# Latent attention: the halves of a head's output copied to one place by ScalarE and added on GpSimd, in place of a matmul by a shift matrix

## The chip, the cores and the metric

The kernel runs on one core of a Trainium2 chip. The time is device time in microseconds (us); the median of three runs of the kernel before is 2149.26 us (2146.79 to 2149.29). Engines are named as in the profile: PE is the matmul engine and PEld its weight loads, DVE is VectorE, ACT is ScalarE, POOL is GpSimd, and SP issues most of the DMAs.

## The reference

The program computes two hybrid decoder layers on 1024 tokens. In each layer three groups of heads run side by side (a gated linear recurrence, latent attention, and cross-attention into 256 memory tokens). Each output is multiplied by a gate, all are put side by side and go through one output projection and a layer norm. The change touches the latent attention alone:

```python
def attend(args):
    qn, qr, blk = args
    s = (jnp.einsum('bqhd,bkhd->bhqk', qn, k_nope)
         + jnp.einsum('bqhr,bkr->bhqk', qr, k_rope)).astype(jnp.float32) * scale
    ...
    s = jnp.where(mask, s, NEG_BIG)
    p = jax.nn.softmax(s, axis=-1).astype(v.dtype)
    return jnp.einsum('bhqk,bkhd->bqhd', p, v)
...
y = jnp.concatenate([y_hg * jax.nn.silu(hg_gate),
                     y_mla * jax.nn.silu(mla_gate),
                     y_mem * jax.nn.silu(mem_gate)], axis=-1)
```

There are 8 heads with values of width 64, and the attention is causal.

## The kernel before, in words

The latent attention of a layer is the function `mla_attend`. It walks 32 steps, 8 heads by 4 pairs of query blocks (`j` = 0 to 3, 256 queries each), in one fixed order.

- `scores` of the next step is written ahead of the rest of a step. For each of the two 128-query blocks PE makes the scores in a PSUM tile A (there are two), DVE takes the row maximum (`nm`, L1041), ACT the exponential and its sum (`pr`, L1044), DVE the reciprocal of the sum (`rs`, L1045), and POOL scales the rows (`pr`, L1048), in chunks of up to 512 columns. A tile A is free for the next scores when its exponential is done.
- `turn` transposes 256 keys by 256 queries of `pr` on PE (L1058) into a PSUM tile B (there are four). ACT rounds them to `ph` (L297) and DVE takes the rest `pl` (L298), so that a product keeps its precision with two matmuls.
- `values` multiplies `ph` and `pl` with the values (L1082, L1083) into one tile B for the whole step. It runs three turns behind (`LAG`). The weights `VV` of a head hold the rounded values in columns 0 to 63 and what is left in columns 64 to 127, so the product holds two halves in partitions 0 to 63 and 64 to 127, and the output is their sum.
- `close` makes that sum. ACT copies the whole product to SBUF (`ol`, L1086, one buffer), and one turn later PE multiplies it with `shift` (L1093), a 128x128 matrix that moves partitions 64 to 127 down by 64, and adds it to the same PSUM tile. DVE multiplies the first 64 partitions with the gate (`yt`, L1096, two buffers), and SP stores the result to HBM (`Yd`, L1097). So each of the 64 steps of the two layers has one copy, one matmul by `shift`, one multiplication and one store.

In the second step of a head the next head's queries are projected (`qf`, then `qh` and `ql` on POOL, L1011 and L1012). Between the last step of a head and the third of the next stand the short steps `j` = 0 and 1, with few products between one score and the next. We call that stretch a head boundary. There are seven in a layer.

A scheduler orders the program: it takes each engine's instructions by their place in the code and by its own estimate of when they are ready. An engine runs its instructions in that order and waits where one is not ready. So removing or adding an instruction also moves others.

Of the kernel before, what the change touches and what calls it, by code (L numbers as in the profile page):

```python
# [7 lines left out]
F32 = mybir.dt.float32  # L8
F32R = mybir.dt.float32r
# [3 lines left out]
ALU = mybir.AluOpType  # L13
# [4 lines left out]
P = 128  # L18
# [23 lines left out]
C_ID = 0  # L42
# [39 lines left out]
def program(tc, xT, xtok, memT, pos, w_in, small, w_uq, w_uk, w_uv, w_mk, w_mv,  # L82
            w_out, ln_g, ln_b, cst, msk, out):
    nc = tc.nc
    es = ExitStack()

    def pool(name, **kw):
        return tc.tile_pool(name=name, **kw)

    cp = es.enter_context(pool("cp", bufs=1))  # L90
# [29 lines left out]
    def T(pl, shape, dt=F32, tag=None, bufs=None):  # L120
        n_name[0] += 1
        return pl.tile(shape, dt, tag=tag, name=f"{tag}_{n_name[0]}", bufs=bufs)
# [4 lines left out]
    def psB():  # L127
        return T(pss.p, [P, 512], F32, "B", 4)

    def f32(t):  # L130
        return t.bitcast(F32)
# [8 lines left out]
    NSM = small.shape[1]  # L140
    sm = T(cp, [P, NSM], F32, "sm")

    shift = T(cp, [P, P], F32R, "shift")
    mhalf = T(cp, [P, 8], F32, "mhalf")
    nc.gpsimd.memset(mhalf, -0.5)
    ones = T(cp, [P, 2], F32, "ones")
# [9 lines left out]
    def constants(lp):  # L156
        cs = T(wpc[1], [P, 2048], F32, "raw", 2)[:, 0:C_N]
        nc.scalar.dma_start(cs, cst)
        nc.scalar.dma_start(sm, small)
        nc.gpsimd.memset(f32(shift), 0.0)  # L160
        nc.scalar.copy(shift[:, 0:64], cs[:, C_ID + 64:C_ID + P])
        nc.scalar.copy(idr, cs[:, C_ID:C_ID + P])
        for i, c in enumerate((C_BE, C_BO)):
            nc.scalar.copy(bias_r[i], cs[:, c:c + P])
        mx = T(lp, [P, HGH], F32, "mx")
        nc.vector.tensor_tensor(out=mx, in0=sm[:, 0:8], in1=sm[:, 8:16], op=ALU.max)
        e = T(lp, [P, 2, HGH], F32, "e")
        for l in range(2):
            nc.vector.tensor_tensor(out=e[:, l], in0=sm[:, 8 * l:8 * l + 8], in1=mx, op=ALU.subtract)
        nc.scalar.activation(e, e, AF.Exp)  # L170
        sme = T(lp, [P, HGH], F32, "sme")
        nc.vector.tensor_tensor(out=sme, in0=e[:, 0], in1=e[:, 1], op=ALU.add)
        nc.vector.reciprocal(out=sme, in_=sme)
        for l in range(2):
            nc.vector.tensor_tensor(out=e[:, l], in0=e[:, l], in1=sme, op=ALU.mult)
        nc.vector.memset(lb[:, 0], 0.0)
        nc.vector.tensor_tensor(out=lb[:, 1], in0=e[:, 0], in1=e[:, 1], op=ALU.add)
        nc.vector.tensor_tensor(out=lb[:, 1], in0=lb[:, 1], in1=e[:, 0], op=ALU.subtract)
        nc.vector.tensor_scalar(out=oml, in0=lb, scalar1=-1.0, scalar2=1.0, op0=ALU.mult, op1=ALU.add)
        return cs  # L180
# [175 lines left out]
    def mem_attn(l, X, tiles, kp):  # L356
        kT, vT, _ = tiles
        with pool(f"m{l}", bufs=1, reuse_waits="tile") as mp:
# [70 lines left out]
            def begin():  # L429
# [45 lines left out]
                for hd in range(2):  # L475
                    part("q", KC - 2, (hd,))
                    part("q", KC - 1, (hd,))
                    evac("q", hd, accs["q", hd])
                mem_in(tiles, mp)
                cs = constants(mp)  # L480
                rope_angles(mp, cs)
                rope_rows(mp)
# [507 lines left out]
    def mla_attend(l, cqT, ckT, KK, uq, kv, k_proj, k_odd, v_proj, rtab, VV, kvr, uqr, lp, rp):  # L990
        uqh, uql = (t.rearrange("p (r c) -> p r c", r=2) for t in uq)
        gs = []
# [71 lines left out]
        opss = {}  # L1064

        def values(hd, j, cp_, ph, pl_):
            hp, ab = hd // 2, hd % 2
            rw = slice(64 * ab, 64 * ab + 64)
            if cp_ == 0:
                opss[hd, j] = psB()  # L1070
            ops = opss[hd, j][:, 0:256].rearrange("p (b q) -> p b q", b=2)
            for c in range(2):
                kb_ = 2 * cp_ + c
                st = P if c == 0 else -P
                w = VV[:, kb_, hd]
                if kb_ == 2 * j + 1:
                    ov, rh, rl = ops[:, 1], ph[:, 2 * P:3 * P], pl_[:, 2 * P:3 * P]
                else:
                    ov = ops
                    rh, rl = (bass.AP(tensor=t.tensor, offset=t.offset + (0 if c == 0 else 3 * P),  # L1080
                                      ap=[list(t.ap[0]), [st, 2], [1, P]]) for t in (ph[:, :], pl_[:, :]))
                nc.tensor.matmul(ov, lhsT=w, rhs=rh, start=kb_ == 0, stop=False)  # L1082
                nc.tensor.matmul(ov, lhsT=w, rhs=rl, start=False, stop=kb_ == 2 * j + 1)  # L1083
            if cp_ == j:
                t = T(lp, [P, 256], F32R, "ol", 1)
                nc.scalar.copy(t, opss[hd, j][:, 0:256])  # L1086
                return t

        def close(hd, j, t):
            hp, ab = hd // 2, hd % 2  # L1090
            rw = slice(64 * ab, 64 * ab + 64)
            ops = opss.pop((hd, j))
            nc.tensor.matmul(ops[:, 0:256], lhsT=shift, rhs=t, start=False, stop=True, skip_group_check=True)  # L1093
            s_ = slice(j * 256, (j + 1) * 256)
            yt = T(lp, [P, 256], F32, "yt", 2)
            nc.vector.tensor_tensor(out=yt[rw], in0=ops[0:64, 0:256], in1=gs[hp][rw, s_], op=ALU.mult)  # L1096
            (nc.gpsimd if hd == 7 and j > 1 else nc.sync).dma_start(Y[8 + hp, rw, s_], yt[rw])  # L1097

        q_proj(0)
# [10 lines left out]
        def step(a):  # L1110
            t = values(*a)
            if ends:
                close(*ends.pop())
            if t is not None:
                ends.append((a[0], a[1], t))
# [29 lines left out]
        if ends:  # L1145
            close(*ends.pop())
# [201 lines left out]
    for l in range(DEPTH):  # L1348
# [4 lines left out]
        ops = latents_out(l, X, tp)  # L1353
# [75 lines left out]
```

## Time and profile before

| What | Value |
|---|---|
| median of the runs | 2149.26 us |
| time of the profiled execution | 2147.82 us |
| its span | 2146.0 us |
| PE busy over the span | 2064.9 us (96%) |
| DVE busy | 1461.1 us (68%) |
| ACT busy | 1009.6 us (47%) |
| POOL busy | 375.5 us (17%) |
| first stage of latent attention | 729 to 890 us of the span |
| second stage | 1804 to 1965 us |

Matmuls are pipelined, so that one of 280 ns may be followed by the next after 120 ns; PE's cost is read from the starts, not from the sum of durations. The shares over the whole span say little about a stage of 161 us, so the stage is read by itself. The median of the runs is 1.44 us above the profiled execution's time.

### The profile page before, as it was taken

Reading aid. Unit: us, or ns where it says so; the run is one execution under the profiler, and the core shown is the slowest. Engines: PE = TensorE matmul, PEld = TensorE weight load, DVE = VectorE, ACT = ScalarE, POOL = GpSimd, SP = SyncE. Lnnn points to the kernel's source line nnn. Section 1 sums busy time; section 2 is a strip of 40 time slices with the busy share of each in tenths; the row PEclk is TensorE's granted clock in tenths of the full one; section 3 lists DMA queues with packets and bytes.
Section 4 is the critical chain, followed back from the end, with each engine's and each line's share of the span. In section 5 each row is a group of like instructions: output and inputs, shape, how many; then the busy total and the mean of one; then the engine's idle time right before and its main releaser. Section 6 shows DMA issues by size and latency. Waiting matters only on the chain. (4 is left out here: it accounts for less than half of the span.)

```text
span 2146.0 us, 30332 instructions
## 1 busy us (share of the span) xinstructions
PE 2064.9 (96%) x11176; PEld 1751.5 (82%) x11176; DVE 1461.1 (68%) x2663; ACT 1009.6 (47%) x1997; POOL 375.5 (17%) x524
## 2 busy tenths in 40 slices
PE   9998999999999899999999989999999998999997
PEld 7887888888888788788787878888888887888886
DVE  6536777777777788566764367777777777886524
ACT  5534443434343777444554344434343437775311
POOL 0212000000001445211101120000000014452202
PEclk9999999999999999999999999999999999999999
DMA  6413201111114301456761131111111134015312
GB/s 201 133 58 119 63 27 60 40 59 40 59 40 153 126 16 38 154 188 230 237 196 52 55 123 55 35 59 40 60 40 54 45 128 151 15 39 190 108 60 79
DMA packets 122100, 194.47 MB, mean 91 GB/s; under 512 B 8608, under 2 KB 90400, under 8 KB 121952
## 3 DMA queue, kind: packets, MB, share of 16 engines
q1 hardware_dynamic: 101488, 149.05, 21.4%
q0 software_dynamic: 8704, 28.58, 3.5%
q10 hardware_dynamic: 11760, 14.90, 2.1%
q8 instruction: 88, 1.44, 0.3%
q14 instruction: 60, 0.49, 0.1%
HBM read 151.09 MB, written 41.42 MB: 90 GB/s over the span
## 5 line engine op out<-in xcount | busy, mean ns | idle before, releaser
L271 PE MATMUL Y<-x,wh 128*128 128x512 f32 x576 | 234.4, 407 | 2.1 <-ACT wh L297 2.1
L273 PE MATMUL Y<-x,wl 128*128 128x512 f32 x576 | 232.9, 404 | 0.0
L272 PE MATMUL Y<-x,wh 128*128 128x512 f32 x576 | 228.3, 396 | 0.0
L252 DVE TENSOR_TENSOR wl<-raw,wh 128x512 fp32r<-128x512 f32 (+4 forms) x214 | 141.5, 707 | 85.0 <-ACT wh L251 84.8
L272 PE MATMUL Y<-t,wh 128*128 128x512 f32 x432 | 170.8, 395 | 0.0
L271 PE MATMUL Y<-t,wh 128*128 128x512 f32 x432 | 170.1, 394 | 0.5 <-ACT pt L710 0.5
L273 PE MATMUL Y<-t,wl 128*128 128x512 f32 x432 | 168.9, 391 | 0.0
L297 ACT CAST wh<-raw 128x512 fp32r<-128x512 f32 (+1 forms) x124 | 72.9, 593 | 192.5 <-DMA raw<-in_w_in 128.2
L251 ACT CAST wh<-raw 128x512 fp32r<-128x512 f32 (+4 forms) x214 | 118.2, 609 | 86.7 <-PE A L272 49.7
L297 ACT CAST wh<-S 128x512 fp32r<-128x512 f32 x144 | 89.0, 622 | 140.9 <-DVE S L695 65.5
L581 PEld LDWEIGHTS B<-Q,r 128*128 128x128 f32 x896 | 115.7, 191 | 38.4 <-issue 12.5
L1048 POOL TENSOR_SCALAR pr<-pr,rs 128x512 f32<-128x512 f32 (+1 forms) x192 | 116.8, 617 | 148.0 <-DVE rs L1045 135.1
L581 PE MATMUL B<-Q,r 128*128 128x128 f32 x896 | 132.2, 291 | 7.6 <-DVE Q L560 6.1
L298 DVE TENSOR_TENSOR pl<-B,ph 128x512 fp32r<-128x512 f32 (+1 forms) x192 | 119.6, 643 | 23.6 <-ACT ph L297 21.0
L298 DVE TENSOR_TENSOR wl<-raw,wh 128x512 fp32r<-128x512 f32 (+1 forms) x124 | 80.7, 655 | 75.4 <-ACT wh L297 74.6
L271 PEld LDWEIGHTS Y<-x,wh 128*128 128x128 f32 x576 | 109.6, 190 | 21.7 <-ACT wh L297 2.9
L273 PEld LDWEIGHTS Y<-x,wl 128*128 128x128 f32 x576 | 109.2, 190 | 21.3 <-DVE wl L298 1.2
L272 PEld LDWEIGHTS Y<-x,wh 128*128 128x128 f32 x576 | 109.5, 190 | 19.5
L1044 ACT ACTIVATE pr<-A,nm 128x128 f32<-128x128 f32 (+7 forms) x128 | 95.6, 748 | 60.8 <-DVE nm L1041 55.4
L297 ACT CAST ph<-B 128x512 fp32r<-128x512 f32 (+1 forms) x192 | 102.7, 553 | 32.0 <-PE B L1058 16.1
L271 PE MATMUL A<-wh,yh 128*128 128x512 f32 x288 | 112.6, 396 | 4.9 <-ACT wh L251 2.6
L298 DVE TENSOR_TENSOR yl<-yr,yh 128x768 fp32r<-128x768 f32 (+1 forms) x44 | 43.5, 997 | 106.9 <-ACT yh L297 106.0
(340 smaller groups left out, 5573.1 us busy)
## 6 DMA issues: line engine op xcount, KB each, us to landing
raw<-in_w_in SPq DMA_DIRECT2D x84, 512.0 KB, 4.6
raw<-in_w_out SPq DMA_DIRECT2D x32, 1024.0 KB, 5.2
yr<-Yd SPq DMA_DIRECT2D x28, 384.0 KB, 4.5
Yd<-r POOLq DMA_DIRECT2D x32, 256.0 KB, 2.6
raw<-in_w_mk SPq DMA_DIRECT2D x8, 512.0 KB, 4.9
raw<-in_w_mv SPq DMA_DIRECT2D x8, 512.0 KB, 4.4
t<-in_xT SPq DMA_DIRECT2D x16, 256.0 KB, 3.5
Yd<-yt POOLq DMA_DIRECT2D x16, 256.0 KB, 2.4
```

The costliest lines, as they stand in the source:

```text
L251: nc.scalar.copy(h[:, a:b], raw[:, a:b])
L252: nc.vector.tensor_tensor(out=lo[:, a:b], in0=raw[:, a:b], in1=f32(h[:, a:b]), op=ALU.subtract)
L271: nc.tensor.matmul(o, lhsT=lh, rhs=rh, start=first, stop=False, **kw)
L272: nc.tensor.matmul(o, lhsT=lh, rhs=rl, start=False, stop=False, **kw)
L273: nc.tensor.matmul(o, lhsT=ll, rhs=rh, start=False, stop=last, **kw)
L297: nc.scalar.copy(h, src)
L298: nc.vector.tensor_tensor(out=lo, in0=src, in1=f32(h), op=ALU.subtract)
L581: nc.tensor.matmul(lp[:, pr * P:(pr + 1) * P], lhsT=xp[:, pr * P:(pr + 1) * P], rhs=q_moving(Q, pr, b), start=True, stop=True)
L1044: nc.scalar.activation(po, sv, AF.Exp, bias=nm, scale=1.0, accum_out=rs)
L1048: nc.gpsimd.tensor_scalar(out=pr[:, c0:c1], in0=pr[:, c0:c1], scalar1=rs, scalar2=0.0, op0=ALU.mult, op1=ALU.add)
```

## The change

The product's halves are no longer added on PE. ACT copies each half by itself (64 partitions, 256 columns) into the two rows of a new SBUF tile `ol`, both at the partitions where the head's output belongs. POOL adds the two, and DVE multiplies the sum with the gate, now from SBUF. `ol` gets two buffers. The matrix `shift` and the two instructions that make it go.

```diff
-    shift = T(cp, [P, P], F32R, "shift")
...
-        nc.gpsimd.memset(f32(shift), 0.0)
-        nc.scalar.copy(shift[:, 0:64], cs[:, C_ID + 64:C_ID + P])
...
             if cp_ == j:
-                t = T(lp, [P, 256], F32R, "ol", 1)
-                nc.scalar.copy(t, opss[hd, j][:, 0:256])
+                t = T(lp, [P, 2, 256], F32, "ol", 2)
+                for i in range(2):
+                    nc.scalar.copy(t[rw, i], opss[hd, j][64 * i:64 * i + 64, 0:256])
+                opss.pop((hd, j))
                 return t
...
-            ops = opss.pop((hd, j))
-            nc.tensor.matmul(ops[:, 0:256], lhsT=shift, rhs=t, start=False, stop=True, skip_group_check=True)
             s_ = slice(j * 256, (j + 1) * 256)
             yt = T(lp, [P, 256], F32, "yt", 2)
-            nc.vector.tensor_tensor(out=yt[rw], in0=ops[0:64, 0:256], in1=gs[hp][rw, s_], op=ALU.mult)
+            nc.gpsimd.tensor_tensor(out=yt[rw], in0=t[rw, 0], in1=t[rw, 1], op=ALU.add)
+            nc.vector.tensor_tensor(out=yt[rw], in0=yt[rw], in1=gs[hp][rw, s_], op=ALU.mult)
```

The order of the instructions moves on every engine of the stage. First, POOL's order at the boundary from the third head to the fourth in the first layer. Before:

```order
L1048 TENSOR_SCALAR pr_1387_7003<-pr_1387_7003,rs_1386_7001 128x512
L1048 TENSOR_SCALAR pr_1387_7003<-pr_1387_7003,rs_1386_7001 128x384
L1048 TENSOR_SCALAR pr_1391_7019<-pr_1391_7019,rs_1390_7017 128x512 x2
L1048 TENSOR_SCALAR pr_1410_7084<-pr_1410_7084,rs_1409_7082 128x128
L1048 TENSOR_SCALAR pr_1414_7096<-pr_1414_7096,rs_1413_7094 128x256
L1048 TENSOR_SCALAR pr_1435_7171<-pr_1435_7171,rs_1434_7169 128x384
```

The same place now (lines of the new file, three below the old ones; numbers of tiles differ by a few):

```order
L1045 TENSOR_SCALAR pr_1390_7024<-pr_1390_7024,rs_1389_7022 128x512 x2
L1093 TENSOR_TENSOR yt_1401_7064<-ol_1395_7043 64x256
L1093 TENSOR_TENSOR yt_1418_7121<-ol_1405_7080 64x256
L1045 TENSOR_SCALAR pr_1409_7091<-pr_1409_7091,rs_1408_7089 128x128
L1045 TENSOR_SCALAR pr_1413_7103<-pr_1413_7103,rs_1412_7101 128x256
L1093 TENSOR_TENSOR yt_1430_7167<-ol_1425_7151 64x256
L1045 TENSOR_SCALAR pr_1434_7179<-pr_1434_7179,rs_1433_7177 128x384
```

Two adds stand one behind the other behind the scaling of the third head's last rows, and a third stands between the scalings of the fourth head's first two steps.

Second, DVE's order at the same boundary. Before:

```order
L1045 RECIPROCAL rs_1386_7001<-rs_1386_7001 128x1
L298 TENSOR_TENSOR pl_1394_7030<-B_1392_7024,ph_1393_7029 128x512
L1096 TENSOR_TENSOR yt_1397_7041<-B_1350_6860,mg_1173_6220 64x256
L1096 TENSOR_TENSOR yt_1402_7059<-B_1395_7033,mg_1174_6222 64x256
L1045 RECIPROCAL rs_1390_7017<-rs_1390_7017 128x1
L298 TENSOR_TENSOR pl_1400_7050<-B_1398_7044,ph_1399_7049 128x512
L298 TENSOR_TENSOR pl_1405_7067<-B_1403_7062,ph_1404_7066 128x384
L1041 TENSOR_REDUCE nm_1408_7081<-A_1407_7076 128x1
L1041 TENSOR_REDUCE nm_1412_7093<-A_1411_7088 128x1
```

And now:

```order
L1042 RECIPROCAL rs_1385_7006<-rs_1385_7006 128x1
L295 TENSOR_TENSOR pl_1393_7035<-B_1391_7029,ph_1392_7034 128x512
L1042 RECIPROCAL rs_1389_7022<-rs_1389_7022 128x1
L295 TENSOR_TENSOR pl_1399_7056<-B_1397_7050,ph_1398_7055 128x512
L1094 TENSOR_TENSOR yt_1401_7064<-yt_1401_7064,mg_1173_6219 64x256
L295 TENSOR_TENSOR pl_1404_7073<-B_1402_7068,ph_1403_7072 128x384
L1038 TENSOR_REDUCE nm_1407_7088<-A_1406_7083 128x1
L1038 TENSOR_REDUCE nm_1411_7100<-A_1410_7095 128x1
```

The first of the two multiplications now stands far ahead, before the `qf` of the projection. The second, of the tile that POOL adds first in the piece above, stands one `pl` later, with the maxima of the fourth head's first step right behind it. Up to the maximum of the second step the order then is `pl`, two `rs`, a multiplication, two `pl`, a multiplication, `pl`.

## Rows read from the trace of the kernel before

**Rows 1.** By stretch: length, busy us of PE PEld DVE ACT POOL, granted clock, DMA

```profile
729.00:890.00 161.00, 155.72 (x1045) 140.69 (x1044) 129.45 (x255) 113.42 (x260) 79.88 (x115) 1.00 0.11 32
1804.00:1965.00 161.00, 154.81 (x1044) 139.93 (x1043) 131.68 (x258) 116.18 (x266) 80.50 (x115) 1.00 0.13 39
```

**Rows 2.** Tile ol: durations (min/median/max), then waits for it (us, times)

```profile
L1086 ACT CAST ol<-B x64: 361/382/421, 729.3 to 1961.5; 128x256 fp32r<-128x256 f32 x64
L1093 PE MATMUL B<-ol,shift x64: 274/331/388, 729.7 to 1962.0; 128*128 128x256 f32 x64
...
  PEld B L1093: 8.4, 18
  PE B L1093: 4.3, 12
```

**Rows 3.** PE in order of time: start, duration, line, operation, tiles

```profile
755.31 0.28 PE L1093 MATMUL B<-ol,shift 128*128 128x256 f32 x1
755.43 0.60 PE L1058 MATMUL B<-idr,pr 128*128 128x128 f32 x4
```

**Rows 4.** ACT in order of time, third head to fourth

```profile
771.68 0.38 ACT L1086 CAST ol<-B 128x256 fp32r<-128x256 f32 x1
771.95 1.14 ACT L1044 ACTIVATE pr<-A,nm 128x1024 f32<-128x1024 f32 x1
...
779.92 0.58 ACT L1044 ACTIVATE pr<-A,nm 128x384 f32<-128x384 f32 x1 [1.52 <-DVE nm L1041]
```

**Rows 5.** Groups by line and shape, POOL: busy us, mean ns

```profile
L1012 POOL TENSOR_TENSOR ql<-qf,qh 128x512 fp32r<-128x512 f32 x32 | 41.8, 1307 | 2.7
L1048 POOL TENSOR_SCALAR pr<-pr,rs 128x128 f32<-128x128 f32 x32 | 11.9, 372 | 11.5 <-DVE rs L1045 10.2 <-PE B L1058 1.2
L1048 POOL TENSOR_SCALAR pr<-pr,rs 128x512 f32<-128x512 f32 x96 | 67.9, 711 | 65.8 <-DVE rs L1045 58.7 <-PE A L1038 5.1 <-PE B L1058 1.1
```

**Rows 6.** DVE in order of time, third head to fourth

```profile
772.55 0.86 DVE L1096 TENSOR_TENSOR yt<-B,mg 64x256 f32<-64x256 f32 x2
...
773.68 1.16 DVE L298 TENSOR_TENSOR pl<-B,ph 128x512 fp32r<-128x512 f32 x2 [0.19 <-ACT ph L297]
...
775.62 0.16 DVE L1045 RECIPROCAL rs<-rs 128x1 f32<-128x1 f32 x1 [0.26 <-ACT pr L1044]
...
777.04 1.95 DVE L298 TENSOR_TENSOR pl<-B,ph 128x512 fp32r<-128x512 f32 x3 [0.18 <-ACT ph L297]
778.90 0.41 DVE L1096 TENSOR_TENSOR yt<-B,mg 64x256 f32<-64x256 f32 x1
779.27 0.56 DVE L1041 TENSOR_REDUCE nm<-A 128x1 f32<-128x384 f32 x1
```

**Rows 7.** POOL in order of time, third head to fourth

```profile
773.65 1.36 POOL L1048 TENSOR_SCALAR pr<-pr,rs 128x512 f32<-128x512 f32 x2 [0.46 <-DVE rs L1045]
```

**Rows 8.** PE in order of time, third head to fourth

```profile
780.67 0.39 PE L271 MATMUL A<-K,qh 128*128 128x320 f32 x1
```

**Rows 9.** DVE and POOL in order of time, around 854 us

```profile
853.78 0.62 POOL L1011 TENSOR_SCALAR qh<-qf 128x512 fp32r<-128x512 f32 x1 [0.17 <-DVE qf L1010]
853.88 1.06 DVE L252 TENSOR_TENSOR wl<-raw,wh 128x512 fp32r<-128x512 f32 x1 [0.19 <-ACT wh L251]
854.49 1.61 POOL L1012 TENSOR_TENSOR ql<-qf,qh 128x512 fp32r<-128x512 f32 x1
...
856.46 0.67 DVE L252 TENSOR_TENSOR wl<-raw,wh 128x512 fp32r<-128x512 f32 x1
```

**Rows 10.** DVE, POOL and PE in order of time, second head to third

```profile
753.53 0.42 DVE L1096 TENSOR_TENSOR yt<-B,mg 64x256 f32<-64x256 f32 x1 [0.19 <-PE B L1093]
...
759.47 1.16 DVE L1041 TENSOR_REDUCE nm<-A 128x1 f32<-128x384 f32 x2
...
753.33 1.36 POOL L1048 TENSOR_SCALAR pr<-pr,rs 128x512 f32<-128x512 f32 x2 [1.43 <-DVE rs L1045]
...
760.85 0.42 PE L271 MATMUL A<-K,qh 128*128 128x320 f32 x1 [0.17 <-ACT pr L1044]
```

## The prediction

> **What bounds the kernel now.** I read the busy time by stretch first, since the change lies in two stages of 161 us each. There PE is busy for 155 us, DVE for about 130, ACT for 115 and POOL for 80, at a granted clock of 1.00 [rows 1]. So PE sets the pace, but DVE has only some 30 us of free time in a stage, and it runs in order. Then I read who waits for `ol`: PE's matmuls wait 4.3 us in all and its weight loads 8.4 us [rows 2]. Last I walked two head boundaries in order of time. There it is not PE that sets the pace. At the third head's end DVE works nearly without a pause from 772.55 to 779.8 [rows 6]. The maximum of the fourth head's second step (128x384) starts at 779.27, its exponential on ACT runs from 779.92 to 780.50 after ACT idled 1.52 us for that maximum [rows 4, 6], and the next scores, which need that exponential's tile A, start on PE at 780.67 [rows 8]. At the second head's end the same matmul waits 0.17 us for that exponential [rows 10]. So at a boundary DVE's chain decides, with 0.2 us to spare or none, and whatever delays that maximum delays PE.
>
> **What the change removes.** 64 matmuls by `shift`, 32 in a layer. Where PE is dense, one takes from 755.31 to the next start at 755.43, 0.12 us [rows 3]: 64 x 0.12 = 7.7 us. With it go the waits for `ol`, between 4.3 us (matmuls) and 8.4 us (weight loads, which overlap other matmuls) [rows 2]; I take 8.4 as the upper end. If nothing became late, the gain would be 12.0 to 16.1 us. The two instructions that made `shift` run at the start beside the first loads, off any wait of the stage; I cost them at nothing.
>
> **ACT.** One copy of 128x256 becomes two of 64x256. The old one lasts 0.38 us, and ACT's next starts 0.27 us after it [rows 2, 4]. The half as many partitions shorten nothing if ACT works by columns, so each layer gains 32 x 0.27 = 8.6 us of ACT, on 115 of 161. The bounds are 0 (partitions halve it) and 32 x 0.38 = 12.2 us. It hides in ACT's idle time, and costs a boundary some 0.25 us, since the `ph` behind the copies comes that much later.
>
> **POOL.** The trace has no add of 64x256. It has a two-input instruction of 128x512 at 1.307 us, and one-input scalings of 0.372 us for 128 columns and 0.711 for 512 [rows 5]. The scalings give (0.711 - 0.372) / 384 = 0.88 ns a column and a fixed 0.26 us. Taking that fixed part out, two inputs cost (1.307 - 0.26) / 512 = 2.05 ns a column, so an add is 0.26 + 256 x 2.05 ns = 0.78 us. Bounds: half of 1.307, 0.65, and the whole, 1.31. I take 0.78, as the fixed part is read from the same engine. Over a layer it is 25 us on 80, still far from full. What counts is what stands ahead of it and behind it.
>
> **DVE, and the new wait.** The multiplication keeps its shape, and its 0.41 us [rows 6]. But it now waits for ACT's copies and POOL's add instead of PE, and everything behind it on DVE waits too: `pl`, the maxima, the reciprocals that POOL's scalings need. I walk the boundary to the fourth head with the new order. POOL is busy with the scaling of two 128x512 chunks from 773.65 to 775.01 [rows 7]; the add comes behind it, to 775.79. DVE has no use for that time: it has done `pl` by 774.55 (start 773.95, 0.27 later than the 773.68 of the row, for the second copy on ACT; `pl` 0.6) and stands at the multiplication until 775.85, a wait of 1.3 us. Up to the 128x384 maximum DVE then does the same work as before plus one multiplication, 0.42 us, which used to end ahead of this piece (of two, 772.55 to 773.41 [rows 6], one moved far ahead, one into it). Two idle gaps of 0.26 and 0.18 us [rows 6] absorb 0.44. So that maximum is 0.27 + 1.3 + 0.42 - 0.44 = 1.55 us later.
>
> To this comes a collision. Around 854 us POOL's `qh` starts at 853.78, and DVE's `wl`, which has two inputs in SBUF, starts 0.10 later and takes 1.06 us, where it takes 0.67 alone; POOL's next then takes 1.61 instead of 1.31 [rows 5, 9]. So such a DVE instruction and a POOL instruction run one after the other, whichever came first. The multiplication had one input in PSUM; now both are in SBUF, and right behind its add POOL has another add or a scaling ready. The Trainium skill has this as a rule: on the page SBUF — State Buffer, under Who interferes with whom, a VectorE instruction with two SBUF inputs and a GpSimd instruction that reads SBUF exclude each other, and the second blocks until the first is done. The trace agrees with it (1.06 beside 0.67 us); by it every multiplication that finds POOL running pays, and without it none would.
>
> At this boundary the second add would be running, 0.78 us. I take one such collision for each boundary, since the two adds stand one behind the other: 1.55 + 0.78 = 2.3 us, less PE's slack of 0.2 (the exponential ends 780.50, the matmul starts 780.67): 2.1 us. The lower bound is 1.35, without a collision. For the upper bound a second collision costs up to 0.78 and POOL's `qh` and `ql` for the next head, which now stand behind an add, shift the scaling by some 0.4: 3.3 us.
>
> At the boundary to the third head the multiplication of the same place ran at 753.53 [rows 10]. POOL scales until 754.69 [rows 10], the add ends at 755.47, and DVE gets there at 754.4 at best: 1.05 us of wait, about 0.05 net for the later copy, 1.1 without a collision and 1.9 with one; up to 2.7 as above. PE had no slack there: it waited 0.17 us already.
>
> **The sum.** A layer has seven boundaries, four like the first and three like the second (those with the next pair's keys): 4 x 2.1 + 3 x 1.9 = 14.1 us lost. The matmuls by `shift` within a boundary, three of four in a head, are gained ahead of the wait and lost in it. The fourth of each head lies in dense PE time: 8 x (0.12 + 8.4 / 64) = 2.0 us gained. Net loss 12.1 us a layer, 24 us for two. On the profiled execution's 2147.82 us that is 2172 us; on the median shown, 1.44 above it, 2173. Bounds: without collisions 2 x (4 x 1.35 + 3 x 1.1 - 2.0) = 13 us, 2162 on the median; at the upper bounds 2 x (4 x 3.3 + 3 x 2.7 - 2.0) = 39 us, 2188.
>
> **What costs nothing.** The end of the stage: the last multiplication and its store are followed by an output projection that reads these rows late. SP issues the first loads of the output weights a few stores earlier; nothing in the stage waited for them, so I give it nothing. A tile B is free once ACT has copied it, earlier than before; PE hardly waits for one.
>
> **The rivals.**
> 1. PE keeps the pace and the change gains. For it: PE is busy 155 of 161 us [rows 1], POOL is half idle and the waits for `ol` vanish [rows 2]. Against it: the maximum at the boundary has no slack [rows 6, 8]. It holds if POOL's first add at a boundary ends before DVE reaches the multiplication, that is, if the scaling ahead of it is over by 773.8 instead of 775.01, or DVE comes there 1.2 us later than in my walk. Price: -12.0 to -16.1 us, 2133 to 2137; with a part of the waits left, up to 2144.
> 2. The two cancel: DVE waits only at some boundaries, or about 1 us at each, as PE's earlier arrival moves the whole chain forward: 2145 to 2153.
> 3. POOL becomes the chain: an add ahead of `qh` and `ql`, longer adds (1.31 us) and more collisions late in the stage, where DVE also splits the output weights (two SBUF inputs each): beyond the upper bound, 2188 to 2200.
>
> **How the numbers follow.** What tells a change from none in this kernel is about 0.2%, 4.3 us. My forecast (2162 to 2188) gets 0.60, rival 1 0.20, rival 2 0.10, rival 3 0.10. Faster by over 0.2% is then 0.20, within it 0.10, slower 0.70. The likeliest case alone has 2162 to 2188; the range that should hold 8 in 10 reaches down into rival 1 and over the edge of rival 3: 2141 to 2191.
>
> **What would show it right or wrong.** In the changed kernel's profile I expect DVE idle before the multiplication (new line 1094) with POOL's add as releaser, by 1 us or more at a boundary and some 15 us or more in both stages; multiplications of up to 1.2 us instead of 0.41 where POOL runs beside them; adds near 0.78 us; ACT's idle time for `nm` before the 128x384 exponential grown from 1.5 us, and PE's wait for that exponential grown from 0.17 to about 2 us, seven times a stage. Both stages should be longer by about 12 us, and all else the same. I am wrong if the stages are shorter, if DVE hardly waits for the add, or if the multiplications stay at 0.41 us throughout.

## The result, and the profile after

The changed kernel takes 2184.86 us (median of 4 runs, 2183.0 to 2188.74), beside 2149.24 us for the kernel before on the same chip: a ratio of 1.0174, 95% interval 1.0159 to 1.0189, or 35.6 us more. The forecast was 2173 us with a range of 2141 to 2191. The sign and the larger part of the place are as forecast; about 12 us of the size are not. The profiled execution took 2183.0 us, its span 2181.2.

Busy time by stretch of the changed kernel (answers to [rows 1]; columns as there):

```profile
729.00:906.00 177.00, 156.81 (x1003) 139.59 (x1002) 132.71 (x254) 128.58 (x294) 102.29 (x146) 0.96 0.10 29
1804.00:1980.00 176.00, 156.64 (x986) 139.57 (x985) 134.96 (x259) 128.29 (x292) 103.65 (x146) 0.96 0.12 38
```

From the first to the last multiplication by `VV` a stage takes 175.7 us in both layers; before, it took 156.2 and 157.2. That is 38.1 us in the two stages; all the rest of the span became 2.8 us shorter. ACT and POOL each gained busy time, DVE hardly, and the granted clock of a stage fell from 1.00 to 0.96.

The three new groups by line and shape (busy us, mean ns of one, then the idle time before them and its releasers):

```profile
L1093 POOL TENSOR_TENSOR yt<-ol 64x256 f32<-64x256 f32 x64 | 48.4, 762 | 15.5 <-ACT ol L1084 13.6
L1084 ACT COPY ol<-B 64x256 f32<-64x256 f32 x128 | 47.1, 368 | 5.8 <-PE B L1080 4.1
L1094 DVE TENSOR_TENSOR yt<-yt,mg 64x256 f32<-64x256 f32 x64 | 33.0, 516 | 39.6 <-POOL yt L1093 39.2
```

DVE stands idle 39.2 us for POOL's add, and its multiplications take 516 ns on average where one takes 0.42 us undisturbed: 64 x (516 - 422) ns = 6 us more.

DVE in order of time, end of the third head to the fourth, the place of [rows 6]:

```profile
769.56 0.56 DVE L295 TENSOR_TENSOR pl<-B,ph 128x384 fp32r<-128x384 f32 x1 [0.20 <-ACT ph L294]
771.54 0.42 DVE L1094 TENSOR_TENSOR yt<-yt,mg 64x256 f32<-64x256 f32 x1 [1.42 <-POOL yt L1093]
771.99 1.28 DVE L1007 TENSOR_TENSOR qf<-B,rtab 64x512 f32<-64x512 f32 x2
...
778.34 0.69 DVE L295 TENSOR_TENSOR pl<-B,ph 128x512 fp32r<-128x512 f32 x1 [0.84 <-ACT ph L294]
780.11 0.95 DVE L1094 TENSOR_TENSOR yt<-yt,mg 64x256 f32<-64x256 f32 x1 [1.08 <-POOL yt L1093]
780.99 0.54 DVE L295 TENSOR_TENSOR pl<-B,ph 128x384 fp32r<-128x384 f32 x1
781.45 0.60 DVE L1038 TENSOR_REDUCE nm<-A 128x1 f32<-128x128 f32 x2
```

POOL over the same time (answers to [rows 7]):

```profile
770.77 0.74 POOL L1093 TENSOR_TENSOR yt<-ol 64x256 f32<-64x256 f32 x1
772.84 0.62 POOL L1008 TENSOR_SCALAR qh<-qf 128x512 fp32r<-128x512 f32 x1 [1.33 <-DVE qf L1007]
...
776.79 2.61 POOL L1045 TENSOR_SCALAR pr<-pr,rs 128x512 f32<-128x512 f32 x4
779.35 1.43 POOL L1093 TENSOR_TENSOR yt<-ol 64x256 f32<-64x256 f32 x2
```

Two waits are to be seen. The second, at 780.11, is the forecast one: POOL scales until 779.4, its add follows, DVE stands 1.08 us, and the multiplication then takes 0.95 us while POOL's next add runs beside it. The first, at 771.54, was not in the sum: the multiplication of the second head's fourth step stands ahead of the `qf` of the fourth head, and waits 1.42 us there. `qf` is late, so are `qh`, `ql` and the four scalings behind them on POOL, and so again the add of the second wait.

PE in order of time, its waits of this stretch (answers to [rows 8] and the PE row of [rows 10]):

```profile
764.65 0.41 PE L268 MATMUL A<-K,qh 128*128 128x320 f32 x1 [0.27 <-ACT pr L1041]
...
776.72 0.55 PE L1055 MATMUL B<-idr,pr 128*128 128x128 f32 x3 [0.50 <-DVE pl L295]
...
781.58 0.66 PE L1055 MATMUL B<-idr,pr 128*128 128x128 f32 x4 [0.85 <-DVE pl L295]
...
783.93 0.39 PE L1079 MATMUL B<-ph,VV 128*128 128x256 f32 x1 [0.67 <-DVE pl L295]
...
787.22 0.42 PE L268 MATMUL A<-K,qh 128*128 128x320 f32 x1 [0.34 <-ACT pr L1041]
```

From the 128x320 score of the third head to that of the fourth it is now 22.57 us; before it was 780.67 - 760.85 = 19.82 [rows 8, 10]. The 2.75 us are spread over several waits, most of them for `pl`, which DVE makes late. Which matmuls of PE waited for `pl` in the whole program (us, times), in the kernel before:

```profile
  PE B L1082: 1.3, 7
```

and in the changed kernel, with its lines three lower:

```profile
  PE B L1055: 16.7, 24
...
  PE B L1079: 7.1, 12
```

PE's matmuls waited 1.3 us for `pl` before, and 23.8 now. The transposes (L1055) need a tile B that DVE's `pl` has finished reading, the products (L1079) need `pl` itself.

Where the time goes is told by three starts on PE: the first 128x320 score of the first head, the same of the eighth head, and the last product of the stage. First layer, before:

```profile
718.68 0.46 PE L271 MATMUL A<-K,qh 128*128 128x320 f32 x1
868.99 0.42 PE L271 MATMUL A<-K,qh 128*128 128x320 f32 x1
884.44 0.28 PE L1083 MATMUL B<-pl,VV 128*128 128x128 f32 x1
```

and after:

```profile
719.37 0.31 PE L268 MATMUL A<-K,qh 128*128 128x320 f32 x1
885.21 0.42 PE L268 MATMUL A<-K,qh 128*128 128x320 f32 x1
904.50 0.27 PE L1080 MATMUL B<-pl,VV 128*128 128x128 f32 x1
```

From the first head's score to the eighth's, a way with all seven boundaries in it, it was 150.31 us and is 165.84, 15.5 more (14.7 in the second layer). From there to the stage's end it was 15.45 us and is 19.29, 3.8 more (the same in the second layer). So 30.3 of the 38.1 us lie in the boundaries and 7.7 at the two ends, where the eighth head's last rows are scaled and no next head follows.

### The profile page after: what moved, and what is told of

The parts are those of the page before. It is cut to its first block, busy times and chain, and to the rows that moved or that the text cites. A ratio compares the mean times of both kernels' runs of the same rounds, so it can differ in the third digit from the quotient of the medians.

```text
span 2181.2 us, 30451 instructions
## 1 busy us (share of the span) xinstructions
PE 2072.4 (95%) x11112; PEld 1753.4 (80%) x11112; DVE 1467.0 (67%) x2663; ACT 1038.2 (48%) x2060; POOL 420.9 (19%) x587
## 4 chain that ended last, share of the span: by engine, by line
PE 33%; DVE 7%; issue 3%; ACT 3%; POOL 2%; DMA 2%; POOLq 0%; ACTq 0%; DVEq 0%
PE Y L268 4%; PE Y L269 4%; PE Y L270 4%; PE A L268 3%; PE A L270 3%; PE A L269 3%; PE B L578 3%; PE B L270 2%; PE B L268 2%; PE B L269 2%; DMA raw<-in_w_in 2%; DVE wl L295 1%; DVE nm L1038 1%; PE B L609 1%; POOL pr L1045 1%
## 5 line engine op out<-in xcount | busy, mean ns | idle before, releaser
L269 PEld LDWEIGHTS Y<-x,wh 128*128 128x128 f32 x576 | 109.6, 190 | 19.5
L1055 PE MATMUL B<-idr,pr 128*128 128x128 f32 x576 | 99.6, 290 | 23.6 <-DVE pl L295 16.7
L290 POOL TENSOR_TENSOR rst<-ss,mhalf 128x4 f32<-128x4 f32 x32 | 36.4, 1138 | 432.9 <-DVE ss L288 414.5
```

What stands on the lines that cost most here:

```text
L269: nc.tensor.matmul(o, lhsT=lh, rhs=rl, start=False, stop=False, **kw)
L290: nc.gpsimd.tensor_tensor(out=r[:, 0:k], in0=ss, in1=mhalf[:, 0:k], op=ALU.pow)
L1055: nc.tensor.transpose(pt[:, k * P:(k + 1) * P], pb[b][:, (2 * cp_ + c) * P:(2 * cp_ + c + 1) * P], ident)
```

## The experiments

Theory 1 was that of the forecast: DVE runs in order, and all that stands behind its multiplication waits for POOL's add. The rivals: ACT's second copy costs by itself (2); POOL's load costs, by late scalings (3); DVE and POOL excluding one another is the larger part (4); PE's lower clock behind its stalls adds to it (5). Differences are medians, each against runs of the kernel before on the same chip (2147.8 to 2149.8).

| Kernel | Median, us | To before, us | Ratio, 95% interval |
|---|---|---|---|
| the change | 2184.86 | +35.6 | 1.0159 to 1.0189 |
| multiplication two turns later | 2174.36 | +26.3 | 1.0103 to 1.0141 |
| multiplication two turns later and tied behind | 2164.07 | +14.3 | 1.0037 to 1.0081 |
| the same, one copy | 2152.58 | +3.8 | 1.0010 to 1.0027 |
| the change, one copy | 2180.55 | +31.7 | 1.0129 to 1.0163 |
| before, two copies | 2164.06 | +16.0 | 1.0052 to 1.0094 |
| before, idle adds on POOL | 2151.95 | +3.9 | 1.0005 to 1.0028 |
| add and multiplication on POOL | 2158.97 | +9.2 | 1.0030 to 1.0060 |
| add and multiplication on DVE | 2167.75 | +18.0 | 1.0063 to 1.0118 |
| one copy, both on DVE | 2160.17 | +10.4 | 1.0031 to 1.0063 |
| one copy, add on DVE, gate on POOL | 2152.73 | +4.7 | 1.0014 to 1.0037 |
| the same, gate behind the scaling | 2154.69 | +5.9 | 1.0016 to 1.0037 |
| before, fourth steps alone changed | 2154.56 | +6.8 | 1.0018 to 1.0040 |

**The wait, taken away in two steps.** First the multiplication later in the code, with two whole turns between it and the add (comments added here; `gate` holds the multiplication and the store):

```diff
-            yt = T(lp, [P, 256], F32, "yt", 2)
+            yt = T(lp, [P, 256], F32, "yt", 4)
...
+            muls.append([0, hd, j, yt])        # in close, behind the add
...
+            while muls and muls[0][0] > 2:     # in step, counted once a turn
+                gate(*muls.pop(0)[1:])
```

> The changed kernel with DVE's gate multiplication (and its store) written two turns behind POOL's add of the same tile; copies, adds and multiplications stay 128, 64 and 64. Theory 1 (DVE runs in order and stands at the multiplication until POOL's add is done, and the transposes' remainders and row maxima behind it come late): DVE's idle time for the add falls from 39 us to under 15, and the time from 2184.9 to 2150-2170 us. Theory 2 (ACT's second copy), 3 (POOL's load, which delays its scalings) and 4 (DVE and POOL excluding one another, whichever waits): the time stays at 2180-2190, since none of these is taken away. Theory 5 (PE's lower clock behind its stalls adds to the loss): stretches at 1.2 GHz in the stage go as far as the waits go.

Measured: 2174.36, above the 2150 to 2170 of theory 1, below the 2180 of the others. DVE still waits:

```profile
  POOL yt L1093: 26.6, 28
```

The scheduler orders by readiness, and left the multiplication ahead of `qf` where it was. Of the 26.6 us, 13.4 stand in the ten waits there, as in the changed kernel. So each multiplication was tied behind the DVE instruction written last ahead of it:

```diff
+            after = [i for i in nc.cur_bb.bb.instructions if i.engine == mybir.EngineType.DVE][-1]
+            with tc.issue_after(after):
                 nc.vector.tensor_tensor(out=yt[rw], in0=yt[rw], in1=gs[hp][rw, s_], op=ALU.mult)
```

> As the first experiment on the changed kernel (multiplication two turns behind the add), but each multiplication is also tied behind the DVE instruction written last ahead of it, so that in DVE's order every multiplication stands one place later: the fourth of a head behind the next head's qf and scores, the third just ahead of the next qf. Copies, adds and multiplications stay as many. Theory 1 (DVE's in-order wait): the wait for the add falls from 39 us to under 6, and the time to 2155-2168 us; what is then left above 2149 is the second copy, which by the run with two copies in the kernel before is worth up to 16 us. Theory 4 (DVE and POOL excluding one another is the larger part): still 2170 or more, with multiplications of 0.9 us. Theory 3 (POOL's load): at least 2170.

Now DVE waits little for the add:

```profile
  POOL yt L1093: 3.4, 2
```

and the time is 2164.07, inside theory 1's 2155 to 2168. No multiplication is stretched any more (452 ns at most). So 21.3 of the 35.6 us go with the wait, though ACT's copies, POOL's adds and DVE's multiplications are as many as in the changed kernel. Theory 3 and theory 4 both had 2170 or more here, and are out as the main cause. The tie ends the waits and the stretching together, so the 21.3 us hold both; of DVE's time the stretching had been 6 us, the waits 39. 14.3 us remain.

**The second copy.** In the kernel before, alone:

```diff
-                nc.scalar.copy(t, opss[hd, j][:, 0:256])
+                for i in range(2):
+                    nc.scalar.copy(t[64 * i:64 * i + 64], opss[hd, j][64 * i:64 * i + 64, 0:256])
```

> The kernel before with ACT's copy made in two halves (64x256 each, 128 copies in all), and nothing else: the matmul by the shift matrix stays, POOL adds nothing. Theory 2 (ACT's second copy is what costs): 2160-2184 us. Theory 1: ACT has 40 us to spare in a stage, and the time is within 4 us of before, 2147-2153.

Measured 2164.06: theory 2's range, and 11 us above theory 1's upper bound. One stretch of the stage, and who waits for `ol` there by the line of the shift matmul:

```profile
730.00:895.00 165.00, 156.12 (x1038) 139.13 (x1036) 130.04 (x254) 127.03 (x294) 80.44 (x115) 1.00 0.10 31
```

```profile
  ACT ol L1087: 23.7, 50
```

The clock stays at 1.00, DVE and POOL are as before, and the waits of PE and its weight loads for `ol` have nearly doubled from 8.4 + 4.3 us [rows 2]. Here the copy is followed by PE, with one `ol` buffer, so part of the price belongs to the matmul that the change removes. Two kernels without that matmul show it apart; both leave out the upper half's copy, and POOL adds the lower half to itself:

```diff
-                for i in range(2):
-                    nc.scalar.copy(t[rw, i], opss[hd, j][64 * i:64 * i + 64, 0:256])
+                nc.scalar.copy(t[rw, 0], opss[hd, j][0:64, 0:256])
...
-            nc.gpsimd.tensor_tensor(out=yt[rw], in0=t[rw, 0], in1=t[rw, 1], op=ALU.add)
+            nc.gpsimd.tensor_tensor(out=yt[rw], in0=t[rw, 0], in1=t[rw, 0], op=ALU.add)
```

> The changed kernel without the copy of the product's upper half: POOL adds the lower half's copy to itself, so the upper half's part is left out of the output. Adds, multiplications and the wait of DVE for POOL are all kept. Theory 2 (the second copy has a price of its own beside the wait, 12-16 us): 2169-2173 us. Theory 1 alone (all of it is the wait): 2178-2185. If the copy is only a delay ahead of the wait, the wait shrinks with it, from 39 to about 25 us.

> The same omission (no copy of the upper half, whose part is left out of the output) in the kernel whose multiplications are tied behind, where DVE hardly waits (3.4 us) and the time is 2164. Theory 2 (what is left above 2149 is the second copy): 2146-2152. Theory 3 (it is POOL's load): 2158-2164, since POOL's 64 adds stay.

Where DVE does not wait, the second copy is worth 14.3 - 3.8 = 10.5 us (2152.58, at the edge of theory 2's range and far from theory 3's). In the changed kernel it is worth 35.6 - 31.7 = 3.9, which is theory 1's range, and within the uncertainty of such a difference (5 us) of nothing: without it the adds come sooner, but DVE waits more, not less. Neither difference is the copy alone: with the same row as both inputs POOL's add is shorter too, 610 ns at the median instead of 732, which is 7.8 us for 64.

```profile
L1092 POOL TENSOR_TENSOR yt<-ol 64x256 f32<-64x256 f32 x64 | 39.1, 614 | 17.6 <-ACT ol L1083 15.7
L1093 DVE TENSOR_TENSOR yt<-yt,mg 64x256 f32<-64x256 f32 x64 | 31.7, 495 | 50.1 <-POOL yt L1092 49.8
```

I had expected the wait to shrink to 25 us; it grew to 49.8. At the boundary walked above the multiplication stands a reciprocal and a `pl` earlier in DVE's order than in the changed kernel, so the scheduler moved the multiplications forward with the copies. Both comparisons say the same thing of the wait: it is the largest part, 21.3 us with two copies and 31.7 - 3.8 = 27.9 with one.

**POOL's load.** In the kernel before, with an add whose result nothing reads:

```diff
+            u = T(lp, [P, 256], F32, "un", 2)
+            nc.gpsimd.tensor_tensor(out=u[rw], in0=f32(t)[rw], in1=f32(t)[rw], op=ALU.add)
```

> The kernel before with 64 additional POOL adds of the changed kernel's size, ol added to itself into a tile that nothing reads (ol has two buffers). Nothing on DVE waits for them. Theory 3 (POOL's load is what costs, by late scalings or by excluding DVE): 2160-2184 us. Theory 1: within 6 us of before, 2147-2155, a part of it from scalings that stand behind an add.

Measured +3.9 us: theory 1's range. The load itself costs a little, since scalings now and then stand behind an add. PE's matmuls waited for the rows `pr` that POOL scales, before

```profile
  PE B L1058: 0.4, 2
```

and with the idle adds

```profile
  PE B L1058: 3.8, 8
```

This kernel has two `ol` buffers instead of one, and PE's matmuls wait 2.9 us for `ol` instead of 4.3; so the load alone may cost somewhat more than 3.9. The kernel with both on POOL

```diff
-            nc.vector.tensor_tensor(out=yt[rw], in0=yt[rw], in1=gs[hp][rw, s_], op=ALU.mult)
+            nc.gpsimd.tensor_tensor(out=yt[rw], in0=yt[rw], in1=gs[hp][rw, s_], op=ALU.mult)
```

> The changed kernel with the multiplication on POOL too, right behind the add: DVE has no part in the output any more and waits for nothing of it, POOL does 128 instructions of 0.73 us instead of 64. Theory 1: DVE's waits are gone and it has 13 us less work in a stage, but POOL's scalings stand behind 1.5 us; 2150-2172 us. Theory 3 (POOL's load): slower than the changed kernel, 2190-2215. Theory 2 (the second copy): 2160 or more whatever POOL does.

says it from the other side: twice the instructions on POOL, and 26 us faster than the change, as nothing on DVE waits for them. It missed theory 2's bound by 1 us (2160 or more; 2158.97).

**DVE instead of POOL.** The add on DVE (`nc.vector` in place of `nc.gpsimd`, nothing else), and then with one copy whose sum starts from PSUM:

```diff
-                    nc.scalar.copy(t[rw, i], opss[hd, j][64 * i:64 * i + 64, 0:256])
+                nc.scalar.copy(t[rw], opss[hd, j][64:128, 0:256])
...
-            nc.vector.tensor_tensor(out=yt[rw], in0=t[rw, 0], in1=t[rw, 1], op=ALU.add)
+            nc.vector.tensor_tensor(out=t[rw], in0=opss.pop((hd, j))[0:64, 0:256], in1=t[rw], op=ALU.add)
             nc.vector.tensor_tensor(out=yt[rw], in0=t[rw], in1=gs[hp][rw, s_], op=ALU.mult)
```

> The changed kernel with the add on DVE instead of POOL, right ahead of the multiplication: two copies on ACT as in the changed kernel, no POOL part, DVE 64 x 0.42 = 27 us more. Theory 1 (the wait for POOL): it goes, and in its place stand 0.42 us more DVE work per step, about half of what the wait and the stretched multiplications took; 2165-2175 us. Theory 2 (the second copy): the copies stay, so 2160 is the least. Theory 3 (POOL's load) and 4 (exclusion): POOL has no add, 2150-2165.

> As the kernel just described, but with one copy of the upper half alone; DVE adds it to the lower half in PSUM and multiplies: no POOL part, no shift matmul, 64 ACT copies less, the DVE work the same. Against the kernel just described the difference is the second copy alone: by theory 2 it is 12-16 us faster than that one, by theory 1 alone 0-5 us. Against the kernel with the gate on POOL (2152.7) it shows what is worth more, 0.42 us more on DVE or 0.73 us on POOL: 2148-2165.

27 us more of DVE work cost less (+18.0, in theory 1's range) than waiting for POOL to do it (+35.6). The second copy is worth 7.6 us here (2167.75 to 2160.17), between the two theories' ranges, and again not the copy alone, as DVE's add then has one input in PSUM. With both on DVE and two copies its two instructions have both inputs in SBUF and take 485 and 487 ns on average, though their medians are 422:

```profile
L1094 DVE TENSOR_TENSOR yt<-yt,mg 64x256 f32<-64x256 f32 x64 | 31.2, 487 | 1.4
L1093 DVE TENSOR_TENSOR yt<-ol 64x256 f32<-64x256 f32 x64 | 31.0, 485 | 7.5 <-ACT ol L1084 6.1
```

**A version that might beat both.** One copy, DVE adds from PSUM, POOL multiplies last, and nothing but the store waits for it:

```diff
+            nc.vector.tensor_tensor(out=t[rw], in0=opss.pop((hd, j))[0:64, 0:256], in1=t[rw], op=ALU.add)
+            nc.gpsimd.tensor_tensor(out=yt[rw], in0=t[rw], in1=gs[hp][rw, s_], op=ALU.mult)
```

> No matmul by the shift matrix, and the two engines' parts exchanged: ACT copies only the upper half (64x256), DVE adds it to the lower half in PSUM, and POOL does the gate multiplication last, behind which only the store waits. Theory 1 (the wait of DVE for POOL is what costs): DVE waits for nothing of POOL, the gain of the removed matmuls shows, and the time is 2132-2146 us. Theory 2 (ACT's second copy): the same, since there is one copy only. Theory 3 (POOL's load): POOL has as many added instructions as in the changed kernel, so the time is 2165-2185. Theory 4 (exclusion of a two-SBUF-input DVE instruction and POOL): DVE's added instruction has one input in PSUM, so most of the loss goes too.

```profile
L1091 DVE TENSOR_TENSOR ol<-B,ol 64x256 f32<-64x256 f32 x64 | 26.3, 412 | 4.5 <-ACT ol L1083 3.6
```

32 us faster than the change, but still 4.7 slower than before, outside the ranges of all theories: DVE waits for nothing of POOL, and the gain of the removed matmuls that I expected did not come. DVE's add, with one input in PSUM, takes 412 ns on average, with no long ones (421 at most). The gain did not come either with the multiplication tied behind POOL's scaling (as above, but with `EngineType.Pool`, `> 1` in place of `> 2`, and four `ol` buffers):

> One copy, DVE's add from PSUM, and the gate multiplication on POOL as in the kernel that took 2152.7 us, but with the multiplication two turns later and tied behind the POOL instruction written last ahead of it, so that it stands behind the scaling of the rows and not ahead of it; ol has four buffers. If POOL's late scalings are what kept that kernel 5 us above before, the time is 2143-2149. If they are not, it stays at 2150-2155.

Measured 2154.69, in the second range: this order of the scalings does not bring the gain. The last run asked whether the matmul is worth anything where the forecast said that it was, in the fourth step of each head:

```diff
+            if j < 3:
                 nc.tensor.matmul(ops[:, 0:256], lhsT=shift, rhs=t, start=False, stop=True, skip_group_check=True)
```

with copy, add and multiplication of the fourth steps as in the kernel of 2152.73 us.

> The kernel before, except that the fourth step of each head (8 closes of a layer, where PE is dense) loses its matmul by shift: ACT copies the upper half alone, DVE adds it to the lower half in PSUM, POOL multiplies with the gate, and nothing but the store waits for POOL. The other 24 closes of a layer stay. The prediction's term for these closes (2.0 us gained per layer) says 2144-2147 us, faster than before by about 4; if the removed matmuls are worth nothing there either, since other work sets the pace, 2148-2151.

Measured +6.8 us, outside both ranges. No kernel tried here beats the one before.

## Why the prediction was right, and where its size was not

**Right: what bounds the boundary.** DVE's in-order chain does. Taking the wait away, and the stretching with it, and leaving all work in place gives back 21.3 us.

**Right in kind, half in size: the wait that was walked.** The walk put the wait at the multiplication of a head's first step, once a boundary: 8.35 us a layer and seven collisions of 0.78, for two layers 16.7 + 10.9 = 27.6. In the trace these fourteen multiplications wait 9.7 us, and ten of them are stretched, by 5.1 us in all: 14.8. The other 29.5 of DVE's 39.2 us stand ahead of multiplications that the walk left out. That the boundaries still lost about what was forecast is therefore partly luck (the sum below).

That DVE and POOL exclude one another is borne out: the multiplication at 780.11 is done at 781.06, only after POOL's second add (779.35 + 1.43 = 780.78), the instructions with two SBUF inputs are stretched (516 ns on average in the changed kernel, 485 and 487 with both on DVE), and the one with an input in PSUM is not (412). The Trainium skill's rule (SBUF — State Buffer, Who interferes with whom) says the same, that a VectorE instruction with two SBUF inputs contends with a GpSimd instruction that reads SBUF; the trace agrees, with 12 of the 64 multiplications over 500 ns. The add has a median of 732 ns beside the 780 worked out, a half copy 368 beside 382 for the whole.

**Mis-sized: the wait ahead of `qf`.** The upper bound had 0.4 us for a late `qh` and `ql`, because they stand behind an add. In the trace the fourth step's multiplication waits ahead of `qf`, ten times 1.34 us. DVE's order, known with the change, has the multiplication "far ahead, before the `qf`", and I counted it as gone from the boundary instead of as a second wait. It is the largest wait that the walk lacked. How much of the time it alone is worth no run tells: the step from 2174 to 2164 us took these 13.4 us away together with 10 others.

**Put at nothing: the end of the stage.** "I give it nothing" was said of the last multiplication and its store, and the sum had seven boundaries a layer. But the eighth head's end has the same waits without being a boundary: from its score to the stage's last product there are 3.8 us more a layer, 7.7 in all. DVE stands 1.04 and 0.85 us for POOL's add there, and the second multiplication is stretched to 0.94 us:

```profile
893.23 0.42 DVE L1094 TENSOR_TENSOR yt<-yt,mg 64x256 f32<-64x256 f32 x1 [1.04 <-POOL yt L1093]
...
898.66 0.94 DVE L1094 TENSOR_TENSOR yt<-yt,mg 64x256 f32<-64x256 f32 x1 [0.85 <-POOL yt L1093]
```

**Wrong: the gain of 2.0 us a layer.** "The fourth of each head lies in dense PE time" was no reason for a gain. With those matmuls gone, and their add on DVE and their gate on POOL, the time rose 6.8 us. Of the 7.0 us by which that kernel's profiled execution is longer, 3.6 lie in the two stages and 3.4 in the rest of the span, whose code the edit does not touch; so there is no gain, but how much of the loss the fourth steps make is open. Where all are gone and DVE hardly waits (one copy, tied behind), PE's matmuls wait for `pl`

```profile
  PE B L1055: 6.8, 10
...
  PE B L1079: 1.5, 4
```

8.3 us, beside 1.3 before, and for POOL's scaled rows `pr`

```profile
  PE B L1055: 10.3, 16
```

beside 0.4 before. Removed were 64 x 0.12 = 7.7 us of matmuls and 4.3 us of waits for `ol`: what PE saves, it waits for DVE and POOL a few matmuls later. PE is busy 97% of the stage [rows 1], and still the engines that make its operands set the pace of this kernel. What the matmuls would be worth with neither late is not shown, as every kernel without them moved their work to DVE or POOL.

**Mis-sized: the second copy.** "It hides in ACT's idle time, and costs a boundary some 0.25 us", of which the walk left 0.05. The differences are 3.9 us in the changed kernel (uncertain by 5), 7.6 to 10.5 where DVE does not wait for POOL, 16 ahead of the shift matmul. No run has its price alone: the first three come with a shorter add, the last with PE's wait for `ol`. ACT's busy share (113 of 161 us) says nothing of it, since `ph` behind the copies is itself on DVE's chain.

**Put at nothing: POOL's load.** The idle adds cost 3.9 us (2151.95). The kernel with one copy, tied behind, has the same load and no shift matmul, and is 3.8 slower than before: this too shows no gain from the 64 matmuls.

**Not in the sum: the clock.** In each stage of the changed kernel three stretches ran at 1.2 GHz, 13.7 us; none did in the kernel before. The rows of the first stage:

```profile
830.00:834.00 4.00, 3.72 (x15) 3.43 (x16) 2.43 (x6) 1.76 (x5) 1.00 (x2) 0.58 0.13 33
851.00:855.00 4.00, 3.53 (x19) 3.33 (x19) 2.78 (x7) 3.43 (x8) 2.78 (x5) 0.57 0.72 229
875.00:882.00 7.00, 5.03 (x25) 4.95 (x25) 4.89 (x11) 4.11 (x11) 4.35 (x7) 0.51 0.58 214
```

and what it does to matmuls of 256 columns:

```profile
877.96 0.41 PE L1080 MATMUL B<-pl,VV 128*128 128x256 f32 x1
878.17 0.41 PE L1079 MATMUL B<-ph,VV 128*128 128x256 f32 x1
```

They start 0.21 us apart instead of 0.12. For all matmuls that start in these stretches without a wait, the distance from the start before, less the median distance of the same shape outside, comes to 5.0 us in the first stage and 4.5 in the second: an estimate of 9.5 us at most, if PE had nothing else to wait for. No run changes the clock alone. In these runs it falls behind PE's stalls and goes with them: 13.7 us a stage at 1.2 GHz in the changed kernel, 10.2 with the multiplication later, 6.8 with it tied behind, 3.4 and none there with one copy.

**The sum again.** By place: the forecast had 28.2 us for the fourteen boundaries, less 3.5 of the gain for the fourth matmuls that lie between them, 24.7; measured are 30.3. It had no loss for the ends of the two stages; measured are 7.7. Each stage is 19.5 and 18.6 us longer instead of 12. So more than half of what was missing lies at a place that the sum left out, and the boundaries came out near the forecast partly by chance: the wait that was walked is half as large, and the waits ahead of `qf` and the lower clock, which the forecast did not have, fill it up.

By cause, in one order: 3.8 us (64 adds on POOL and no shift matmul, DVE hardly waiting, one copy), plus 27.9 for the wait, plus 3.9 for the second copy, is 35.6. In the other order (the copy first, 10.5, then the wait, 21.3) the parts shift by 6.6 us: wait and copy share a chain and do not add. Each part is a difference of two kernels, and by their intervals uncertain by 2 to 6 us; that the wait is the largest holds in either order, the shares of the rest do not stand so firm.

**Wrong: where PE would wait.** I expected its wait for the 128x384 exponential to grow from 0.17 to 2 us; it is 0.27 and 0.34. PE was held one step earlier, by `pl`. The observable was mistaken, not the chain: both come from the same late DVE.

## What to carry to other kernels

Before moving work to an idle engine, ask who waits for its answer in order: 64 adds on POOL cost 3.9 us when nothing waited for them, and taking DVE's wait for them away gave back 21 to 28. Walk every place where the new wait stands, the end of the stage too, and not only the one where the chain is known to be tight; a multiplication moved out of one critical stretch here landed ahead of another. And a matmul taken from an engine that is 97% busy was no gain here, where other engines make its operands just in time.

## What the runs showed of the hardware that was not expected

- PE's clock fell to 1.2 GHz while PE was still busy for most of the time. In the 7 us ahead of the three stretches it was busy 5.46, 5.49 and 5.32 us, with single waits of at most 1.68 us; PE of the kernel before was busy 6.79 to 7.00 us in the same three windows of time, and kept 2.4 GHz.
- A POOL add of 64x256 takes 732 ns (median) from two different rows of `ol`, and 610 with the same row as both inputs (idle adds, and the two kernels that add the lower half to itself).
- ACT's copy of 256 columns from PSUM takes 368 ns (median) for 64 partitions in the kernel before with two copies, and 382 for 128 in the kernel before: half the partitions save 14 ns.
